# Two of the first loads' sources move to ScalarE's queue: block 1's first token half and the second weight granule

## The chip, the cores and the metric

The kernel runs on one core of a Trainium2 chip. Its five engines work side by side, each through its own instructions in a fixed order: TensorE (PE in the profile, with its weight loads as PEld), VectorE (DVE), ScalarE (ACT), GpSimd (POOL) and SyncE (SP), which here only issues DMAs. A DMA that an engine issues is carried out by 16 DMA engines that all queues of the core share. The metric is the device time of one execution in microseconds (us); lower is better.

## The reference

Two layers of a decoder trunk over 256 tokens of width 1024, all in float32. Each layer is a mixer followed by a gated feed-forward part, both between RMS norms with a residual:

```python
def rmsnorm(x, g):
    y = xf * lax.rsqrt(jnp.mean(xf * xf, axis=-1, keepdims=True) + RMS_EPS)
    return (y * g.astype(F32)).astype(x.dtype)

def hybrid_mixer(h, w_in, ...):
    proj = h @ w_in                       # 1024 x 3088
    aq, ak, av, gq, gk, gv, gr, g_low = jnp.split(proj, cuts, axis=-1)
    ...                                   # attention over aq, ak, av; gated linear attention over the rest
    return mixed @ w_out

def swiglu(h, w_gate, w_up, w_down):
    return (jax.nn.silu(h @ w_gate) * (h @ w_up)) @ w_down

def reference(x, ...):
    h = x
    for l in range(DEPTH):                # DEPTH = 2
        m = hybrid_mixer(rmsnorm(h, mix_pre_norm[l]), ...)
        h = h + rmsnorm(m, mix_post_norm[l])
        f = swiglu(rmsnorm(h, ffn_pre_norm[l]), w_gate[l], w_up[l], w_down[l])
        h = h + rmsnorm(f, ffn_post_norm[l])
    return h
```

## The kernel before

The 256 tokens lie in two blocks of 128 rows, `h[0]` and `h[1]` (h0 and h1 in the profile's order rows: h_87 and h_88). A weight matrix comes in granules of two times 128 rows by 512 columns (512 KB): each granule is loaded into one of four buffers `raw`, and then split for a product of float32 accuracy. ScalarE writes the rounded part `wh`, VectorE the remainder `wl` = weight - `wh`; in the first layer both multiply with a column of the norm's gain, `gcol`, on the way, a row half (128 rows) at a time. Tokens are transposed on TensorE (`tp_x`, four transposes for 512 columns), then split in the same way into `xh_x` (ScalarE) and `xl_x` (VectorE). A product is three matmuls: xh times wh, xh times wl, xl times wh. The first product is `aq`, the queries: 4 granules x 2 row halves x 2 token blocks x 3 = 48 matmuls of 512 columns; granules 0 and 1 need the first 512 columns of the tokens, granules 2 and 3 the last. `gqk`, `ak`, `gr`, `gv`, `av` and `wo` follow, then the feed-forward part.

Before the first product the gain has to be there: `grow`, a 16 x 128 table (8 KB), is loaded, transposed on TensorE (`tp_gain`) and copied by ScalarE into `gcol`. Every `wh` and `wl` of the first granules reads `gcol`. TensorE also runs two bursts of matmuls on zeros, `warm` (`NWARM`, 6 and 3 calls), one before `tp_gain` and one between the first and the second `tp_x`.

The order on each engine is not written by hand. A class `Clock` keeps a modelled time for each engine; generators for the tasks (`first_x`, `highs`, `lows_`, `project`, ...) are woken at modelled times and emit their instructions then. So a change of the first loads also changes what the planner emits next, on all engines, until its modelled times agree again. `Engine.__getattr__` charges every call to the engine's name; all objects named "DMA" share one modelled queue. `load_x(j, i)` (line 1412) loads half i of token block j, `load_plain(i)` (line 338) granule i, and `grow_of` (line 1408) the gain table. The first three granules are loaded as two DMAs of 256 KB each (`NSTEP` = 3). A granule from the fifth on waits for its buffer, that is for the `wl` of the granule four before it. The first loads are issued by lines 1416 to 1424, all on SP's queue.

Of the kernel before, what the change touches and what calls it, by code (L numbers as in the profile page):

```python
# [21 lines left out]
P = 128  # L22
# [34 lines left out]
class Engine:  # L57


    def __init__(self, clock, name, eng):  # L60
        self.clock, self.name, self.eng = clock, name, eng
# [46 lines left out]
class Clock:  # L108
# [5 lines left out]
    def __init__(self, nc):  # L114
        self.at = dict.fromkeys(("PE", "Act", "DVE", "Pool", "DMA"), 0.0)
        self.idle = 0.0
        self.queue = 0.5
        self.free = {}
        self.port = {}
        self.writes = {}  # L120
        self.last = {}
        self.slots = {}
        self.open = set()
        self.tasks = []
        self.pumps = []
        self.count = 0
        self.pe = Engine(self, "PE", nc.tensor)
        self.act = Engine(self, "Act", nc.scalar)
        self.dve = Engine(self, "DVE", nc.vector)
        self.pool = Engine(self, "Pool", nc.gpsimd)  # L130
        self.dma = Engine(self, "DMA", nc.sync)

    @staticmethod
    def span(ap):
# [103 lines left out]
def trunk(ctx: ExitStack, tc: tile.TileContext, io: dict):  # L238
    nc = tc.nc
# [6 lines left out]
    ck = Clock(nc)  # L246
    pe, act, dve, pool, dma, close = ck.pe, ck.act, ck.dve, ck.pool, ck.dma, ck.close
# [54 lines left out]
    for l in range(L):  # L302
        w_in, w_out = io["w_in"][l], io["w_out"][l]
        for name in ("gqk", "aq", "ak", "gr", "gv", "av") if l else ("aq", "gqk", "ak", "gr", "gv", "av"):
            if name == "gqk":
                add((l, name), [w_in[:, 1536:2048], w_in[:, 3072:3088]], 8, 528, None if l else 0)
            else:
                c0 = {"aq": 0, "ak": 512, "gr": 2560, "gv": 2048, "av": 1024}[name]
# [26 lines left out]
    lows = [0]  # L335
    plain_lows = [0]

    def load_plain(i):
        key, k0, kk, n, srcs = queue[i]
        raw = wpool.tile([P, kk, n], F32, tag="raw", bufs=NRAW, name="raw")  # L340
        if len(raws) >= NRAW:
            ck.after(raw, raws[-NRAW])
        step = 1 if len(raws) < NSTEP else kk
        for k in range(0, kk, step):
            c0 = 0
            for src in srcs:
                w = src.shape[1]
                r0 = (k0 + k) * P
                dma.dma_start(raw[:, k:k + step, c0:c0 + w],
                              src[r0:r0 + step * P, :].rearrange("(k p) n -> p k n", p=P))  # L350
                c0 += w
        raws.append(raw)
        raw_of[i] = raw

    def loader(first):
        for what, at_, *src in loads[first:]:
            if what == "plain":
                while len(raws) >= plain_lows[0] + NRAW:
                    yield ck.now() + 0.1
                load_plain(at_)  # L360
                continue
            f = forms[at_]
            while at_[0] not in (mixed_all if what in ("b11", "b21") else sums_of):
                yield ck.now() + 0.1
            t = yield from ck.tile(sb, [P, 4, 512], F32, "big", NBIG, what)
            if src[0] is not None:
                fw = src[0].shape[1]
                for g in range(2):
                    dma.dma_start(t[:, 2 * g:2 * g + 2, 0:fw],
                                  src[0][256 * g:256 * (g + 1), :].rearrange("(k p) n -> p k n", p=P))  # L370
            f["tiles"][what] = t
            if what in ("b11", "b21", "b22"):
                f["ready"][what] = t
# [1009 lines left out]
            then = pre_norm(j, xout, l + 1) if l + 1 < L else None  # L1383
            ck.spawn(post_norm(j, acc[j], gi, then), ck.now())

    act.preload_act_table_set("natural_log_exp_and_others")

    warm = sb.tile([P, P], F32, tag="ra", bufs=1, name="warm")
    dve.memset(warm, 0.0)
# [14 lines left out]
    h = [const.tile([P, D], F32, name=f"h{j}") for j in range(2)]  # L1404
# [3 lines left out]
    def grow_of(name, t):  # L1408
        dma.dma_start(t, io[name].rearrange("l (k p) -> (l k) p", p=P))
        return t  # L1410

    def load_x(j, i):
        c = slice(i * 512, (i + 1) * 512)
        dma.dma_start(h[j][:, c], io["x"][0, j * P:(j + 1) * P, c])

    load_x(0, 0)
    grow = grow_of("mix_pre_norm", sb.tile([16, P], F32, tag="lsig", bufs=1, name="grow"))
    load_plain(0)
    load_x(1, 0)
    load_plain(1)  # L1420
    load_x(0, 1)
    load_x(1, 1)
    for i in range(2, 4):
# [91 lines left out]
```

## Time and profile before

| What | Value |
|---|---|
| Time, three runs | 642.36, 639.14, 641.89 us; median 641.89 us |
| Profiled execution | 639.99 us, its span 638.2 us |
| TensorE busy | 622.1 us, 97% of the span |
| VectorE busy | 504.3 us, 79% |
| ScalarE busy | 412.6 us, 65% |
| GpSimd busy | 23.7 us, 4% |
| Moved by DMA | 109.30 MB, mean 171 GB/s |

All times within the profile count from the start of the span; the execution's own time is 1.8 us longer than its span. Busy is the time in which an engine has an instruction at work; for TensorE the ends of matmuls are modelled, so its 97% says that something was in its pipeline, not that it computed at its peak. A row of a timeline gives start, duration, engine, line, operation, result and sources, and in square brackets how long the engine stood idle before and what released it. Line L77 is the helper through which every operation is recorded, so groups are told apart by their tiles.

### The profile page before, as it was taken

To read this page: it belongs to the slowest core of one execution; us is meant where nothing else is said; L and a number is where in the kernel's file an instruction comes from. 1 tells how busy PE (TensorE), PEld (TensorE's weight loads), DVE (VectorE), ACT (ScalarE), POOL (GpSimd) and SP (SyncE) were. 2 spreads that over 40 slices of the span, in tenths; PEclk is the share of its full clock that TensorE was granted. 3 is DMA by queue.
4 is the path that set the end of the run, shared out by engine and by line. 5 is a ranking of instruction groups with operands and counts; after the bars stand their busy time and mean duration, and the time that the engine had idled before them with its cause. 6 is when DMAs were issued, how large, how long until landed. Compare 5 with 4: busy or idle time off the path is not lost.

```text
span 638.2 us, 10255 instructions
## 1 busy us (share of the span) xinstructions
PE 622.1 (97%) x3896; PEld 510.7 (80%) x3896; DVE 504.3 (79%) x784; ACT 412.6 (65%) x700; POOL 23.7 (4%) x41
## 2 busy tenths in 40 slices
PE   8999999989999999999999999999899999999995
PEld 7987778868888888879788777887788888888894
DVE  4899975579897899987588996557899778989743
ACT  6889855486946385656577797537966555838531
POOL 1000021000000000000010000110000000000000
PEclk9999999979999999999999999999899999999998
DMA  8965455156048946039474714840910895710811
GB/s 281 281 193 156 149 188 191 52 174 255 1 142 294 397 152 201 1 104 289 142 246 149 205 46 126 277 142 17 368 45 3 286 353 216 270 61 1 263 68 66
DMA packets 53108, 109.30 MB, mean 171 GB/s; under 512 B 5890, under 2 KB 10692, under 8 KB 53060
## 3 DMA queue, kind: packets, MB, share of 16 engines
q1 hardware_dynamic: 53060, 108.66, 51.4%
q8 instruction: 30, 0.49, 0.3%
q14 instruction: 18, 0.15, 0.1%
HBM read 107.60 MB, written 1.05 MB: 170 GB/s over the span
## 4 chain that ended last, share of the span: by engine, by line
PE 86%; DVE 5%; DMA 3%; ACT 3%; issue 2%; SPq 1%; POOLq 0%; DVEq 0%; ACTq 0%
PE dn L77 17%; PE seven_a L77 10%; PE gate_ps L77 8%; PE up_ps L77 8%; PE seven_b L77 7%; PE wo L77 4%; PE gr L77 4%; PE gqk L77 4%; PE ak L77 4%; PE gv L77 3%; PE av L77 3%; PE aq L77 3%; DVE wl L77 3%; ACT wh L77 2%; PE att_o L77 2%
## 5 line engine op out<-in xcount | busy, mean ns | idle before, releaser
L77 DVE TENSOR_TENSOR wl<-raw,wh 128x1024 fp32r<-128x1024 f32 (+1 forms) x124 | 150.3, 1221 | 32.4 <-ACT wh L77 31.6
L77 ACT ACTIVATE wh<-raw 128x1024 fp32r<-128x1024 f32 (+1 forms) x124 | 130.0, 1059 | 54.1 <-DMA raw<-w_gate 17.3
L77 ACT ACTIVATE wh<-b 128x1024 fp32r<-128x1024 f32 x72 | 75.0, 1058 | 38.2 <-PE up_ps L77 9.3
L77 DVE TENSOR_TENSOR wl<-b,wh 128x1024 fp32r<-128x1024 f32 x72 | 84.9, 1218 | 2.9 <-ACT wh L77 2.8
L77 PE MATMUL dn<-wh,xh_h 128*128 128x512 f32 x176 | 70.4, 400 | 0.0
L77 PE MATMUL dn<-wl,xh_h 128*128 128x512 f32 x176 | 69.5, 395 | 0.0
L77 PE MATMUL dn<-wh,xl_h 128*128 128x512 f32 x176 | 69.1, 393 | 0.0
L77 DVE TENSOR_TENSOR b<-b,b 128x1024 f32<-128x1024 f32 x36 | 42.7, 1217 | 0.0
L77 POOL TENSOR_TENSOR rstd<-var,nhalf 128x1 f32<-128x1 f32 (+1 forms) x24 | 21.2, 883 | 557.6 <-DVE var L77 557.5
L77 PEld LDWEIGHTS dn<-wl,xh_h 128*128 128x128 f32 x176 | 33.1, 188 | 8.2 <-DVE wl L77 1.4
L77 PEld LDWEIGHTS dn<-wh,xl_h 128*128 128x128 f32 x176 | 33.0, 188 | 7.4
L77 PEld LDWEIGHTS dn<-wh,xh_h 128*128 128x128 f32 x176 | 33.1, 188 | 7.0
L77 DVE SCALAR_TENSOR_TENSOR wl<-raw,gcol,wh 128x512 fp32r<-128x512 f32 (+1 forms) x48 | 34.4, 748 | 1.6 <-ACT wh L77 1.6
L77 ACT ACTIVATE wh<-raw,gcol 128x512 fp32r<-128x512 f32 (+1 forms) x48 | 32.4, 717 | 4.7 <-DMA raw<-w_in 3.3
L77 PE MATMUL gate_ps<-wh,xh_x 128*128 128x512 f32 (+1 forms) x96 | 34.9, 363 | 0.0
L77 PE MATMUL up_ps<-wh,xh_x 128*128 128x512 f32 (+1 forms) x96 | 34.3, 358 | 0.0
L77 PE MATMUL gate_ps<-wh,xl_x 128*128 128x512 f32 (+1 forms) x96 | 34.1, 356 | 0.0
L77 PE MATMUL gate_ps<-wl,xh_x 128*128 128x512 f32 (+1 forms) x96 | 34.1, 355 | 0.0
L77 PE MATMUL up_ps<-wh,xl_x 128*128 128x512 f32 (+1 forms) x96 | 34.1, 355 | 0.0
L77 PE MATMUL up_ps<-wl,xh_x 128*128 128x512 f32 (+1 forms) x96 | 34.1, 355 | 0.0
L77 ACT ACTIVATE xh_h<-tp_h 128x512 fp32r<-128x512 f32 (+1 forms) x24 | 13.3, 554 | 25.1 <-PE tp_h L77 24.9
L77 DVE TENSOR_TENSOR xl_h<-tp_h,xh_h 128x512 fp32r<-128x512 f32 (+1 forms) x24 | 15.5, 645 | 14.9 <-ACT xh_h L77 14.8
(233 smaller groups left out, 1483.9 us busy)
## 6 DMA issues: line engine op xcount, KB each, us to landing
raw<-w_in SPq DMA_DIRECT2D x45, 512.0 KB, 4.6
raw<-w_down SPq DMA_DIRECT2D x44, 512.0 KB, 4.9
b<-w_gate SPq DMA_DIRECT2D x24, 512.0 KB, 8.2
b<-w_up SPq DMA_DIRECT2D x24, 512.0 KB, 7.5
raw<-w_gate SPq DMA_DIRECT2D x20, 512.0 KB, 4.4
raw<-w_up SPq DMA_DIRECT2D x20, 512.0 KB, 4.8
raw<-w_out SPq DMA_DIRECT2D x16, 512.0 KB, 3.7
raw<-w_in SPq DMA_DIRECT2D x6, 256.0 KB, 5.1
```

The lines of the kernel that those rows point to most:

```text
L77: return f(*args, **kw)
```

## The change

A second object named "DMA" is made whose instructions go to ScalarE's queue (`ck.dma2`), and `load_x` and `load_plain` take the queue as an argument. Block 1's first token half and granule 1 (its two row halves) are issued by ScalarE, ahead of its activation-table load, which moves behind them. On SP's queue granule 0 moves ahead of the gain table, and the other loads follow.

```diff
@@ -129,6 +129,7 @@
         self.dma = Engine(self, "DMA", nc.sync)
+        self.dma2 = Engine(self, "DMA", nc.scalar)
@@ -335,7 +336,7 @@
-    def load_plain(i):
+    def load_plain(i, q=dma):
@@ -346,7 +347,7 @@
-                dma.dma_start(raw[:, k:k + step, c0:c0 + w],
+                q.dma_start(raw[:, k:k + step, c0:c0 + w],
                               src[r0:r0 + step * P, :].rearrange("(k p) n -> p k n", p=P))
@@ -1383,7 +1384,6 @@
-    act.preload_act_table_set("natural_log_exp_and_others")
@@ -1409,15 +1409,16 @@
-    def load_x(j, i):
+    def load_x(j, i, q=dma):
         c = slice(i * 512, (i + 1) * 512)
-        dma.dma_start(h[j][:, c], io["x"][0, j * P:(j + 1) * P, c])
+        q.dma_start(h[j][:, c], io["x"][0, j * P:(j + 1) * P, c])
 
     load_x(0, 0)
+    load_x(1, 0, ck.dma2)
+    load_plain(0)
+    load_plain(1, ck.dma2)
+    act.preload_act_table_set("natural_log_exp_and_others")
     grow = grow_of("mix_pre_norm", sb.tile([16, P], F32, tag="lsig", bufs=1, name="grow"))
-    load_plain(0)
-    load_x(1, 0)
-    load_plain(1)
     load_x(0, 1)
     load_x(1, 1)
     for i in range(2, 4):
```

**SP's and ScalarE's first rows.** SP before, from its first DMA on; h_87 is token block 0, h_88 token block 1, and each of these DMAs but `grow` carries 256 KB (the last row 512 KB each):

```order
L77 DMA h_87<-x 128x512
L77 DMA grow<-mix_pre_norm 16x128
L77 DMA raw<-w_in 128x512 x2
L77 DMA h_88<-x 128x512
L77 DMA raw<-w_in 128x512 x2
L77 DMA h_87<-x 128x512
L77 DMA h_88<-x 128x512
L77 DMA raw<-w_in 128x512 x2
L77 DMA raw<-w_in 128x2x512 x2
```

SP with the change, from its first DMA on; the names have moved by one, so h_86 is block 0 and h_87 block 1:

```order
L77 DMA h_86<-x 128x512
L77 DMA raw<-w_in 128x512 x2
L77 DMA grow<-mix_pre_norm 16x128
L77 DMA h_86<-x 128x512
L77 DMA h_87<-x 128x512
L77 DMA raw<-w_in 128x512 x2
L77 DMA raw<-w_in 128x2x512
L77 DMA rope<-rope 128x64
```

The gain table stands fourth instead of second on SP, behind three DMAs of 256 KB, and three DMAs are gone from SP. ScalarE before, from its first instruction on:

```order
L77 ACT_TABLE_LOAD
L77 ACTIVATE gcol<-tp_gain 128x16
L77 ACTIVATE xh_x<-tp_x 128x512
L77 ACTIVATE wh<-raw,gcol 128x512 x3
L77 ACTIVATE xh_x<-tp_x 128x512
L77 ACTIVATE wh<-raw,gcol 128x512
L77 ACTIVATE xh_x<-tp_x 128x512
L77 ACTIVATE wh<-raw,gcol 128x512
L77 ACTIVATE xh_x<-tp_x 128x512
```

ScalarE with the change, from its first instruction on:

```order
L77 DMA h_87<-x 128x512
L77 DMA raw<-w_in 128x512 x2
L77 ACT_TABLE_LOAD
L77 ACTIVATE gcol<-tp_gain 128x16
L77 ACTIVATE wh<-raw,gcol 128x512
L77 ACTIVATE xh_x<-tp_x 128x512
L77 ACTIVATE wh<-raw,gcol 128x512
L77 ACTIVATE xh_x<-tp_x 128x512 x2
L77 ACTIVATE wh<-raw,gcol 128x512 x2
L77 ACTIVATE sq,ms<-h_87 128x1024
L77 ACTIVATE xh_x<-tp_x 128x512
L77 ACTIVATE sq,ms<-h_86 128x1024
```

Three DMA issues stand ahead of the table load, two splits of block 1's tokens run together, and one of the two sums of squares (`sq`) has moved ahead of the last split of block 0's tokens.

**TensorE's and VectorE's first rows.** TensorE before, from its first matmul on:

```order
L77 MATMUL warm<-warm 128x128 x6
L77 MATMUL tp_gain<-ident,grow 128x16
L77 MATMUL tp_x<-ident,h_87 128x128 x4
L77 MATMUL warm<-warm 128x128 x3
L77 MATMUL tp_x<-ident,h_88 128x128 x4
L77 MATMUL aq<-wh,xh_x 128x512
L77 MATMUL aq<-wl,xh_x 128x512
L77 MATMUL aq<-wh,xl_x 128x512
L77 MATMUL aq<-wh,xh_x 128x512
L77 MATMUL aq<-wl,xh_x 128x512
L77 MATMUL aq<-wh,xl_x 128x512
L77 MATMUL tp_x<-ident,h_87 128x128 x4
```

TensorE with the change, from its first matmul on:

```order
L77 MATMUL warm<-warm 128x128 x6
L77 MATMUL tp_gain<-ident,grow 128x16
L77 MATMUL tp_x<-ident,h_86 128x128 x4
L77 MATMUL warm<-warm 128x128 x3
L77 MATMUL tp_x<-ident,h_87 128x128 x8
L77 MATMUL tp_x<-ident,h_86 128x128 x4
L77 MATMUL aq<-wh,xh_x 128x512
L77 MATMUL aq<-wl,xh_x 128x512
```

All four groups of token transposes, the second halves of both blocks too, stand ahead of the first matmul of `aq`; before, two of the four stood behind it. VectorE before, from its second instruction on:

```order
L77 TENSOR_TENSOR xl_x<-tp_x,xh_x 128x512
L77 SCALAR_TENSOR_TENSOR wl<-raw,gcol,wh 128x512 x2
L77 TENSOR_TENSOR xl_x<-tp_x,xh_x 128x512
L77 SCALAR_TENSOR_TENSOR wl<-raw,gcol,wh 128x512 x2
L77 TENSOR_TENSOR xl_x<-tp_x,xh_x 128x512 x2
```

VectorE with the change, from its second instruction on:

```order
L77 TENSOR_TENSOR xl_x<-tp_x,xh_x 128x512 x3
L77 SCALAR_TENSOR_TENSOR wl<-raw,gcol,wh 128x512 x2
L77 TENSOR_TENSOR xl_x<-tp_x,xh_x 128x512
L77 TENSOR_SCALAR var<-ms 128x1
L77 SCALAR_TENSOR_TENSOR wl<-raw,gcol,wh 128x512 x2
```

The `wl` of granule 0 stands behind three token splits instead of one. Further on TensorE's order differs in the first mixer alone, where shorter pieces change places (among them `av`, the gated attention of block 1 and its transposes `tp_g`); from the middle of `wo` of the first layer to the end the order of both programs is the same.

## Rows read from the trace of the kernel before

**Rows 1.** The page, parts 1 and 4: busy time, and the chain that ended last

```profile
PE 622.1 (97%) x3896; PEld 510.7 (80%) x3896; DVE 504.3 (79%) x784; ACT 412.6 (65%) x700; POOL 23.7 (4%) x41
PE 86%; DVE 5%; DMA 3%; ACT 3%; issue 2%; SPq 1%; POOLq 0%; DVEq 0%; ACTq 0%
```

**Rows 2.** Windows: stretch, length, busy us (instructions) by engine, PEclk, DMA share, GB/s

```profile
2.00:5.00 3.00, 3.00 (x15) 2.74 (x14) 0.00 (x0) 0.20 (x2) 0.27 (x1) 1.00 0.92 222
7.50:10.00 2.50, 2.10 (x13) 1.51 (x12) 0.97 (x2) 1.78 (x3) 0.00 (x0) 1.00 1.04 385
20.00:100.00 80.00, 80.00 (x848) 65.04 (x847) 67.87 (x186) 64.56 (x149) 3.64 (x4) 1.00 0.62 199
```

**Rows 3.** The chain that ended last, in order of time: start us, us, what

```profile
4.00 5.52 DMA h<-x
...
11.43 9.03 PE aq L77 x39
20.46 3.30 PE gqk L77 x27
```

**Rows 4.** Timeline of SP's queue from 0 us

```profile
0.74 0.39 SPq L77 DMA_DIRECT2D h<-x  x1
1.18 0.41 SPq L77 DMA_DIRECT2D grow<-mix_pre_norm  x1
1.65 0.88 SPq L77 DMA_DIRECT2D raw<-w_in  x2
```

**Rows 5.** The tile grow, its DMA alone

```profile
DMA to landing us min/median/max: 2.4/2.4/2.4
```

**Rows 6.** Timeline of TensorE, 1 to 21 us

```profile
1.05 2.93 PE L77 MATMUL warm<-warm 128*128 128x128 f32 x12 [1.05 <-DVE warm L77]
3.91 0.28 PE L77 MATMUL tp_gain<-ident,grow 16*128 16x16 f32 x1
4.12 1.11 PE L77 MATMUL tp_x<-ident,h 128*128 128x128 f32 x4
5.03 1.49 PE L77 MATMUL warm<-warm 128*128 128x128 f32 x6
7.61 0.49 PE L77 MATMUL aq<-wh,xh_x 128*128 128x512 f32 x1
9.66 0.63 PE L77 MATMUL tp_x<-ident,h 128*128 128x128 f32 x4 [0.40 <-DMA h<-x]
20.07 0.39 PE L77 MATMUL aq<-wh,xl_x 128*128 128x512 f32 x1
```

**Rows 7.** Timeline of ScalarE, 0 to 21 us

```profile
0.73 1.28 ACT L77 ACT_TABLE_LOAD   x1 [0.73 <-PEq L1503]
4.23 0.18 ACT L77 ACTIVATE gcol<-tp_gain 128x16 f32<-128x16 f32 x1 [2.22 <-PE tp_gain L77]
8.22 0.73 ACT L77 ACTIVATE wh<-raw,gcol 128x512 fp32r<-128x512 f32 x1 [1.13 <-DMA raw<-w_in]
10.32 0.60 ACT L77 ACTIVATE xh_x<-tp_x 128x512 fp32r<-128x512 f32 x1 [0.29 <-PE tp_x L77]
12.61 1.04 ACT L77 ACTIVATE sq<-h 128x1024 bf16<-128x1024 f32 x1
```

**Rows 8.** Timeline of VectorE, 0 to 21 us

```profile
6.51 1.42 DVE L77 SCALAR_TENSOR_TENSOR wl<-raw,gcol,wh 128x512 fp32r<-128x512 f32 x2
11.39 1.43 DVE L77 TENSOR_TENSOR xl_x<-tp_x,xh_x 128x512 fp32r<-128x512 f32 x2
```

**Rows 9.** Timeline of TensorE, late in the first mixer

```profile
107.71 0.66 PE L77 MATMUL tp_g<-ident,gon 128*128 128x128 f32 x4 [0.77 <-DVE gon L77]
```

**Rows 10.** Windows at the two starts of the feed-forward part, columns as in rows 2

```profile
136.20:143.00 6.80, 6.13 (x15) 4.62 (x15) 5.16 (x7) 4.90 (x13) 0.36 (x1) 0.50 0.89 256
450.20:453.60 3.40, 3.40 (x9) 2.63 (x8) 3.13 (x5) 2.40 (x6) 0.00 (x0) 0.50 0.91 311
```

## The prediction

> **What bounds the kernel now.** I read the page's busy table and chain first: TensorE is at work 97% of the span, and 86% of the chain that ended last runs through it [rows 1]. A chain of this kind says that a delay at the start comes out at the end, if TensorE never waits long enough in between to catch it up. So I looked next at windows: from 20 to 100 us TensorE is busy 80.00 of 80.00 us, with VectorE at 67.87 and ScalarE at 64.56 [rows 2]. Nothing there can swallow a delay. The first place with a real wait is at 107.7 us, 0.77 us long [rows 9]. Then the start itself, by the chain in order of time and the three timelines: the chain begins with a DMA, the second half of a token block that is issued at 4.00 and lands at 9.52, and from 11.43 on it is `aq`, 39 matmuls in 9.03 us, 0.2315 us each, which ends at 20.46 where `gqk` takes over [rows 3]. `aq` began at 7.61 and starts its last matmul at 20.07 [rows 6]; 48 matmuls without a hole would need 11.1 us, so it loses 1.6 us to holes and to the two groups of transposes in it. What counts is therefore one number: when the last `aq` matmul starts.
>
> **How the first data arrive.** The gain table lands 2.4 us after its issue at 1.18 [rows 4, 5], at 3.6; `tp_gain` begins at 3.91 and `gcol` at 4.23 [rows 6, 7]. The 256 KB loads behind it land in the order of issue: the first half of granule 1, which is the fourth 256 KB load after the first, lets `wh` begin at 8.22 [rows 7], and the load two places later lands at 9.52 [rows 3], so one load per 0.65 us. That puts the sixth large load (granule 1's second half) at 8.9 and the eighth (block 1's second half) at 10.2. The DMA engines are the limit by then: 385 GB/s at a share of 1.04 between 7.5 and 10 us. Between 2 and 5 us they carry 222 GB/s at a share of 0.92 [rows 2]: held up, though not for want of issues, since SP issues one load per 0.45 us [rows 4].
>
> **The change part by part.**
>
> *The issues.* SP loses three issues of about 0.44 us, ScalarE gains three. On ScalarE they come before the table load: 0.73 + 1.3 + 1.28 = 3.3 us for its end, against 2.0 now [rows 7]. Nothing needs ScalarE before `gcol`, which needs the gain table, so this costs nothing; even with the gain table at its old 3.6 it would be covered, by 0.9 us.
>
> *The gain table.* It is now SP's fourth DMA, behind block 0's first half and both halves of granule 0, while ScalarE's queue holds three loads of the same size. No row shows two queues loaded at once, so I bound it. At best only SP's own queue counts: the first load lands by 3.6, two more at 0.65 us each, 4.9. At worst all six loads come first at today's pace: 8.9. If the second queue fills the slow stretch, 3 us x (385 - 222) GB/s = 0.49 MB are won, 1.3 us at 385 GB/s: 7.6. Both queues are filled from 0.74 us at one pace, so I take the six, with most of that gain: 7.8. The eighth large load, with the same 1.1 us gained, lands at 9.1 (bounds 8.9 to 10.2): its place in the bytes has not changed.
>
> The Trainium skill (DMA: Bandwidth & Descriptors, "Queues, rings and completion order") says that each DMA engine takes turns between the queues that have work, and under "Issuing engines are not separate DMA queues" that issuing from several engines saves only issue time. By these the gain table stays behind all six loads and nothing of the slow stretch is won: 8.9, and the sum below grows by 1.1 us. No run here has shown it yet.
>
> *From the gain table to the first `aq` product.* Every step has a row. `tp_gain` 0.3 after the landing: 8.1. The second `warm` burst ends 2.6 after that start (3.91 to 6.52 today [rows 6]): 10.7, and only then block 1's first transposes. Their `xh_x` starts 0.66 later (9.66 to 10.32 [rows 6, 7]), 11.36; the second `xh_x` in the pair at 11.96, to 12.56. VectorE now has three `xl_x` ahead of `wl`; the third ends 0.7 after its `xh_x` (two take 1.43 [rows 8]): 13.25. The first `wl` of granule 0 takes 0.71 (two in 1.42 [rows 8]): 13.95. It ends at 7.2 today. The second matmul of `aq` cannot start before 13.95. The first matmul, ahead of it, waits for nothing later than that.
>
> *One more hole.* ScalarE goes on after 12.56 with two `wh` (1.4, to 14.0), then `sq` of block 1 (1.04 [rows 7], to 15.0), then the last `xh_x` (to 15.6); VectorE's `xl_x` of it (16.3) and the first `wl` of granule 1 (17.0) follow. TensorE reaches that granule's second matmul, the 14th, at 13.95 + 12 x 0.2315 = 16.7 and gets it at 17.05. From there 34 starts more: 17.05 + 34 x 0.2315 = 24.9 for the last `aq` start, against 20.07: **4.9 us later**. With 4.9 for the gain table the eighth load decides: landed at 8.9, `xh_x` at 9.9, `wl` ends 11.85, 2.1 us earlier, so 2.8 us later than today in all. With 8.9 it is 6.0.
>
> *The next granules.* The fifth load now stands behind three smaller ones on SP and waits for the `wl` of granule 0, ended at 14.7. With a landing some 5.5 us later (4.00 to 9.52 [rows 3]) it is there at 20.2 and split by 23, ahead of 25. No second wait. The later granules follow at the pace of `wl`, as now.
>
> *Rest of the first mixer.* The pieces that change places are the same work; TensorE is full there, so they cost nothing unless one comes before its data. At 107.7 us the wait of 0.77 us may go, because block 1's gated attention now stands earlier against `av`. I take half: -0.4, between -0.8 and, if such a wait appears elsewhere, +0.8.
>
> *TensorE's clock.* The first four `tp_x` take 1.11 us, later ones 0.63 [rows 6]: the array runs at its lower level (1.2 GHz) at first, though the column of the windows has 1.00 there [rows 2]. Today `warm`, `tp_gain` and `tp_x` keep it at work from 1.05 to 6.5. With the change it stands idle from 4.0 (end of the first `warm` burst) to 8.1, then works to 10.7 and again has holes up to 13.95. So `aq` may begin at 1.2 GHz. The rows show low stretches of 6.8 and 3.4 us at a granted 0.50 [rows 10]. From nothing (high before 13.95) to 6.8 us low from there, half of it lost: 0 to +3.4; I take +0.6, nearer to none, since the second burst and 12 transposes run before.
>
> **The sum.** +4.9 - 0.4 + 0.6 = +5.1 us on the profiled execution's 639.99 us (span 638.2): 645.1. That execution lies 1.9 below the median of the three timed ones, 641.89; the four average 640.9. I add to the average: **646.0 us**.
>
> **Rivals.**
>
> *The gain table slips through.* If SP's queue is served before ScalarE's, it lands near 4.9 and the eighth load decides: +2.8 - 0.4 + 0.6, 643.9. For it: a table of 8 KB needs no bandwidth. Against: three large loads stand ahead in the same queue, and today's loads land in order of issue.
>
> *The clock stays low into `aq`.* +4.9 - 0.4 + 3.4: 648.8. For it: 4.1 us of idleness where none was. Against: `warm` runs again right before.
>
> *Nothing is lost.* The delay is caught up before the end: some wait that the windows do not show gives it back, about 641. Against it stands the full TensorE from 20 to 100 us.
>
> *Faster.* The start costs 2.8, and the two low stretches at 136 and 450 us are missed, because the feed-forward parts begin at another moment: they cost 6.8 / 2 = 3.4 and 3.4 / 2 = 1.7 us [rows 10], and 0.8 us comes from 107.7: 640.9 + 2.8 - 5.1 - 0.8 = 637.8. For it: two starts of the same kind have low stretches of different length, so their length is not fixed. Against: the order of work ahead of them is as before, and both stretches have to go. To come out faster (below 638.7, see below) more than 640.9 + 2.8 - 0.8 - 638.7 = 4.2 of these 5.1 us must be won; less only softens the loss.
>
> **How the numbers follow.** My forecast has 0.50 (643.5 to 648.5 by itself), the gain table that slips through 0.20, the low clock 0.17, nothing lost 0.07, faster 0.06. A measurement of this kernel can tell about 0.5%, 3.2 us, from no change: faster is below 638.7, slower above 645.1. Slower: three quarters of the forecast, all of the low clock, a fifth of the first rival, 0.58. Faster 0.07, with a little for the timed runs' own scatter of 3.2 us; no change 0.35. The range runs from 641 to 650, from nothing lost to the low clock with the table at 8.9.
>
> **What would show it.** Right: `gcol` starts near 8.4 instead of 4.23; TensorE idle from 4.0 to 8; the first `wl` of granule 0 ends near 14; the last `aq` start near 25; from there TensorE's rows of the first mixer follow in the same distance, and `wo` ends some 4 to 5 us later. Wrong: `gcol` at 5 to 6 (the queues are not shared evenly), a first `aq` before 11, or `aq` late but the start of the feed-forward part not later.

## The result, and the profile after

The changed kernel takes 644.63 us (median of 18 runs, 641.24 to 647.62); the kernel before, on the same chip, 640.66 us (18 runs, 638.42 to 644.39). The ratio is 1.0064 with a 95% interval of 1.0049 to 1.0080: slower by 4.1 us, between 3.1 and 5.1. The forecast was 646.0.

The profiled execution took 643.37 us (span 641.6), 3.4 more than the one of before. Its busy times are those of before [rows 1], to within 1 us per engine:

```profile
PE 621.5 (97%) x3896; PEld 510.8 (80%) x3896; DVE 503.6 (79%) x784; ACT 412.0 (64%) x700; POOL 22.7 (4%) x41
```

So nothing became dearer; TensorE did the same work later. The beginning, first by the queues. SP's queue, timeline of the changed kernel (start us, us, what):

```profile
0.74 0.38 SPq L77 DMA_DIRECT2D h<-x  x1
1.18 0.89 SPq L77 DMA_DIRECT2D raw<-w_in  x2
2.11 0.43 SPq L77 DMA_DIRECT2D grow<-mix_pre_norm  x1
```

ScalarE, the same stretch and on to its first activation:

```profile
0.73 0.41 ACTq L77 DMA_DIRECT2D h<-x  x1
1.17 0.93 ACTq L77 DMA_DIRECT2D raw<-w_in  x2
2.14 1.28 ACT L77 ACT_TABLE_LOAD   x1 [2.14 <-issue]
8.52 0.18 ACT L77 ACTIVATE gcol<-tp_gain 128x16 f32<-128x16 f32 x1 [5.10 <-PE tp_gain L77]
```

The two queues do issue side by side, and the table load ends at 3.42, long before anything needs ScalarE. The chain in order of time says what the start now hangs on:

```profile
2.11 5.99 DMA grow<-mix_pre_norm
8.10 0.14 issue
8.23 0.25 PE tp_gain L77
8.48 1.04 PE tp_x L77 x4
9.53 1.28 PE warm L77 x6
10.81 1.72 PE tp_x L77 x8
12.55 0.60 ACT xh_x L77
```

Before, the chain began with a 256 KB token load [rows 3]. Now it is the gain table, 8 KB, 5.99 us from issue to landing (2.4 before [rows 5]). TensorE's timeline shows what follows from it:

```profile
8.23 0.25 PE L77 MATMUL tp_gain<-ident,grow 16*128 16x16 f32 x1 [4.25 <-DMA grow<-mix_pre_norm]
...
13.49 0.48 PE L77 MATMUL aq<-wh,xh_x 128*128 128x512 f32 x1
14.59 0.50 PE L77 MATMUL aq<-wl,xh_x 128*128 128x512 f32 x1 [0.62 <-DVE wl L77]
...
25.37 0.39 PE L77 MATMUL aq<-wh,xl_x 128*128 128x512 f32 x1
```

The last `aq` matmul starts at 25.37 against 20.07 [rows 6], 5.3 us later. From the second `aq` matmul on they follow at about 0.23 us without a hole: (25.37 - 14.59) / 46 starts = 0.234. VectorE shows why the second matmul waits until 14.59: three `xl_x` stand ahead of the first `wl`, which ends at about 14.5.

```profile
10.20 0.69 DVE L77 TENSOR_TENSOR xl_x<-tp_x,xh_x 128x512 fp32r<-128x512 f32 x1 [9.20 <-ACT xh_x L77]
12.33 0.69 DVE L77 TENSOR_TENSOR xl_x<-tp_x,xh_x 128x512 fp32r<-128x512 f32 x1 [1.44 <-ACT xh_x L77]
13.18 0.69 DVE L77 TENSOR_TENSOR xl_x<-tp_x,xh_x 128x512 fp32r<-128x512 f32 x1 [0.16 <-ACT xh_x L77]
13.79 1.41 DVE L77 SCALAR_TENSOR_TENSOR wl<-raw,gcol,wh 128x512 fp32r<-128x512 f32 x2
```

How the delay goes on is read from one tile. The products `seven_a` stand in both feed-forward parts; the two numbers behind the durations are the starts of the first and of the last of these 48 instructions. Changed kernel:

```profile
L77 PE MATMUL seven_a<-wh,xh_x x48: 387/395/628, 141.5 to 593.4; 128*128 128x512 f32 x48
```

Before:

```profile
L77 PE MATMUL seven_a<-wh,xh_x x48: 389/395/628, 135.7 to 589.9; 128*128 128x512 f32 x48
```

So the delay is 5.3 us at the end of `aq`, 5.8 at the start of the first feed-forward part and 3.5 near the end of the second. Four things lie between. TensorE, full from 20 to 100 us before [rows 2], now has three waits there:

```profile
28.29 0.63 PE L77 MATMUL tp_heads<-ident,qk_sb 128*128 128x128 f32 x4 [0.35 <-DVE qk_sb L77]
...
35.97 0.27 PE L77 MATMUL ltp<-ident,qks 128*17 128x128 f32 x1 [0.77 <-ACT qks L77]
...
65.27 0.97 PE L77 MATMUL score<-khl,q 64*128 64x256 f32 x6 [0.37 <-DVE nmax L77]
```

Together they are 1.5 us. The wait of 0.77 us at 107.7 [rows 9] is gone: `tp_g` follows `av` at once (108.62 + 0.23 = 108.85).

```profile
108.62 0.39 PE L77 MATMUL av<-wh,xl_x 128*128 128x512 f32 x1
108.85 0.60 PE L77 MATMUL tp_g<-ident,gon 128*128 128x128 f32 x4
```

The low stretch (a stretch at a granted clock of about 0.5) at the first feed-forward part is 3.4 us instead of 6.8 [rows 10]; the one at the second part is 3.4 us long, as it was. What the first is worth can be read from two starts, the first `seven_a` on `xh_x` and the first on `sums_h`: they lie 32.85 us apart before (135.66 to 168.51) and 31.53 with the change (141.53 to 173.06), 1.3 us less. The second of these rows, before and then with the change:

```profile
168.51 0.40 PE L77 MATMUL seven_a<-wh,sums_h 128*128 128x512 f32 x1
```

```profile
173.06 0.40 PE L77 MATMUL seven_a<-wh,sums_h 128*128 128x512 f32 x1
```

Windows of the changed kernel (columns as in rows 2):

```profile
2.00:5.00 3.00, 1.98 (x10) 1.69 (x8) 0.00 (x0) 1.28 (x1) 0.28 (x1) 1.00 0.87 267
...
14.00:16.00 2.00, 1.41 (x6) 1.14 (x7) 1.27 (x3) 2.00 (x5) 0.00 (x0) 1.00 0.00 0
20.00:100.00 80.00, 78.51 (x830) 63.42 (x830) 68.06 (x189) 64.00 (x147) 1.84 (x4) 1.00 0.57 175
...
142.60:146.00 3.40, 3.02 (x7) 2.44 (x8) 3.39 (x5) 2.39 (x6) 0.00 (x0) 0.51 0.94 330
```

And the profile of before has a wait on TensorE that the changed one has not:

```profile
306.79 0.44 PE L77 MATMUL tp_h<-ident,sg 128*128 128x128 f32 x2 [1.00 <-DVE sg L77]
```

5.3 + 1.5 - 0.8 - 1.3 - 1.0 = 3.7, against 3.4 by the two spans; the rest lies in smaller differences. Which of these belong to the change, and which to the single execution, the experiments have to say.

### The profile page after: what moved, and what is told of

Same layout as the page of the kernel before. It is cut to its first block, busy times and chain, and to the rows that moved or that the text cites. A ratio compares the mean times of both kernels' runs of the same rounds, so it can differ in the third digit from the quotient of the medians.

```text
span 641.6 us, 10253 instructions
## 1 busy us (share of the span) xinstructions
PE 621.5 (97%) x3896; PEld 510.8 (80%) x3896; DVE 503.6 (79%) x784; ACT 412.0 (64%) x700; POOL 22.7 (4%) x41
## 4 chain that ended last, share of the span: by engine, by line
PE 87%; DVE 4%; ACT 4%; DMA 2%; issue 2%; SPq 0%; POOLq 0%; DVEq 0%; ACTq 0%
PE dn L77 19%; PE seven_a L77 11%; PE gate_ps L77 9%; PE up_ps L77 9%; PE seven_b L77 8%; PE wo L77 4%; PE gv L77 4%; PE av L77 3%; PE gr L77 3%; PE gqk L77 2%; PE ak L77 2%; PE aq L77 2%; DVE wl L77 2%; PE att_o L77 2%; ACT wh L77 2%
```

## Experiments

Each ratio is against runs of the kernel before on the same chip. The change does three things at once: two loads go through another queue, the gain table moves from second to fourth place on SP's, and the order in which the engines split tokens and weights changes with the planner's due times. The diffs leave out what they share with the change (`ck.dma2` and the queue argument). My theory was that the late gain table makes the loss and the queues as such nothing; the rival was that the second queue itself costs.

**The queues alone.** The kernel before, with the gain table still second on SP, and the two loads on ScalarE's queue, ahead of its table load. The engines' order is that of before.

```diff
-    load_x(1, 0)
-    load_plain(1)
+    load_x(1, 0, ck.dma2)
+    load_plain(1, ck.dma2)
+    act.preload_act_table_set("natural_log_exp_and_others")
```

> Order of every compute engine as before the change; only block 1's first half and granule 1 are issued by ScalarE, and the gain table stays SP's second DMA. Theory (the loss is the gain table's late landing and the engines' order that follows from it): the gain table lands near 4, the last aq start lies between 19 and 20.5 us, the time is that of the kernel before, -1 to +0.5 us. Rival (a second queue itself slows the first loads, by sharing the DMA engines): the loads on SP land later, the time is 2 to 4 us above before.

Measured: 640.26 us (12 runs) against 640.51 (23), ratio 1.0000 (0.9977 to 1.0022). The rival falls. TensorE's timeline:

```profile
5.46 0.26 PE L77 MATMUL tp_gain<-ident,grow 16*128 16x16 f32 x1 [1.49 <-DMA grow<-mix_pre_norm]
...
20.84 0.39 PE L77 MATMUL aq<-wh,xl_x 128*128 128x512 f32 x1
```

The gain table is second on SP in both kernels and lands at 5.33 here, at 3.6 before, where I had expected it near 4: the other queue's loads take their part of the same DMA engines. The Trainium skill (DMA: Bandwidth & Descriptors, "Queues, rings and completion order") says that the engines take turns between queues that have work, and the trace agrees by these 1.7 us: with SP's queue served first the table would have landed as before. Under "Issuing engines are not separate DMA queues" it says that issuing from several engines saves only issue time; that too agrees, by the ratio of 1.0000. The last `aq` starts at 20.84, 0.77 later than before and above the 19 to 20.5 that I had expected; the time does not show it within its interval.

**The order alone.** The changed kernel, all loads on SP's queue.

```diff
-    load_x(1, 0, ck.dma2)
+    load_x(1, 0)
     load_plain(0)
-    load_plain(1, ck.dma2)
+    load_plain(1)
```

> Order of every compute engine as with the change, but all loads on SP's queue, in the order of the changed code: the gain table is the seventh DMA there. Theory: the gain table lands at 8.9 (six large loads at the pace of the kernel before), the first wl of granule 0 ends near 15.3, the time is 4.5 to 6 us above before, about 1 us above the change. Rival (the second queue makes the loss): the time is that of before, within 1 us.

Measured: 647.91 us (6 runs), ratio 1.0094 (1.0061 to 1.0126). The gain table is now seventh in one queue, issued at 3.53, and its product starts at 8.93:

```profile
8.93 0.25 PE L77 MATMUL tp_gain<-ident,grow 16*128 16x16 f32 x1 [4.95 <-DMA grow<-mix_pre_norm]
...
25.59 0.39 PE L77 MATMUL aq<-wh,xl_x 128*128 128x512 f32 x1
```

The last `aq` starts at 25.59, 0.22 later than with two queues. The whole loss is there without the second queue. Whether that queue wins back anything in time is not settled: the two intervals overlap, and the traces speak for 0.2 us. The profiled execution is the shortest of the six, 642.55 us; only its start is read here.

**The gain table late, the order of before.** One queue, the table's DMA issued behind both granules; the planner books it where it was, so that the engines' order stays.

```diff
-    grow = grow_of("mix_pre_norm", ...)
+    grow = sb.tile(...)
+    gsrc = io["mix_pre_norm"].rearrange(...)
+    ck.note("DMA", dma.cost("dma_start", [grow], {}), [gsrc], [grow])
     load_plain(0)
     load_x(1, 0)
     load_plain(1)
+    nc.sync.dma_start(grow, gsrc)
```

> Order of every compute engine as before the change, one queue; the gain table is issued behind granule 1, as SP's seventh DMA. Theory: it lands near 8.9, the first wl of granule 0 ends near 12, and as all tokens and granules 0 to 2 have landed by then aq runs without a hole: last start near 23.7, 3 to 5 us above before. Rival (the engines' order alone makes the loss): within 1 us of before.

Measured: 645.72 us (6 runs), ratio 1.0077 (1.0055 to 1.0099), 4.9 us (3.5 to 6.3).

```profile
8.55 0.25 PE L77 MATMUL tp_gain<-ident,grow 16*128 16x16 f32 x1 [4.58 <-DMA grow<-mix_pre_norm]
...
24.25 0.39 PE L77 MATMUL aq<-wh,xl_x 128*128 128x512 f32 x1
```

The late table alone costs 4.2 us at the last `aq`, and the time follows.

**The gain table early, the order of the change.** The changed kernel, with the table's DMA issued second on SP and booked at its late place.

```diff
     load_x(0, 0)
+    grow = sb.tile(...)
+    gsrc = io["mix_pre_norm"].rearrange(...)
+    nc.sync.dma_start(grow, gsrc)
     load_x(1, 0, ck.dma2)
     load_plain(0)
     load_plain(1, ck.dma2)
-    grow = grow_of("mix_pre_norm", ...)
+    ck.note("DMA", dma.cost("dma_start", [grow], {}), [gsrc], [grow])
```

> Order of every compute engine and both queues as with the change, but the gain table is issued as SP's second DMA, as before the change. Theory: the table lands near 4.5 and no longer decides; block 1's second half (the eighth large load) does: it lands near 8.9 to 9.3, the first wl of granule 0 ends near 12, the last aq start near 23, the time is 1.5 to 3 us above before. Rival 1 (the gain table alone makes the loss): within 0.7 us of before. Rival 2 (the engines' order alone makes it): as the change, 4 us above.

Measured: 644.58 us (12 runs), ratio 1.0051 (1.0031 to 1.0070), 3.3 us (2.0 to 4.5), a little above what I had expected. Here the table is early, as in the prediction's rival of the table that slips through. As that rival said, the eighth load then decides:

```profile
5.41 0.26 PE L77 MATMUL tp_gain<-ident,grow 16*128 16x16 f32 x1 [1.43 <-DMA grow<-mix_pre_norm]
...
9.51 0.63 PE L77 MATMUL tp_x<-ident,h 128*128 128x128 f32 x4 [0.66 <-DMA h<-x]
...
12.21 0.54 PE L77 MATMUL aq<-wl,xh_x 128*128 128x512 f32 x1 [0.89 <-DVE wl L77]
...
24.51 0.39 PE L77 MATMUL aq<-wh,xl_x 128*128 128x512 f32 x1
```

The last `aq` is 4.4 us late, of which some 1.6 come from a low stretch that this execution has in `aq`: between 12.55 and 15.96 eight starts take 3.41 us, 0.43 apart instead of 0.23. Without it 2.8, as in the prediction.

```profile
12.50:15.90 3.40, 3.40 (x9) 2.64 (x9) 2.67 (x7) 3.40 (x8) 1.05 (x2) 0.51 0.55 155
```

So the late table and the order each hold back the same `aq` matmuls. By the last start they cost 4.2 and 2.8 us by themselves and 5.3 together: they do not add, since one delay hides most of the other. The times (4.9, 3.3 and 4.1 us) have intervals too wide to rank them. Part of the 3.3 is the clock: an estimate like the one at the end of this section leaves 2.6.

**The table load first.** The queues alone, with ScalarE's table load ahead of its DMAs.

```diff
-    load_x(1, 0)
-    load_plain(1)
+    load_x(1, 0, ck.dma2)
+    load_plain(1, ck.dma2)
```

The table load stays where the kernel before has it, ahead of all loads.

> Order of every compute engine as before the change; ScalarE issues block 1's first half and granule 1, but behind its table load, so from about 2.0 us on; the gain table is SP's second DMA. Theory (two queues fill the slow stretch of the DMA engines between 3 and 5 us, but delay the gain table when both start together): the gain table lands at 3.6 as before, the eighth large load near 9 instead of 10.2, the last aq start between 19.0 and 19.8 us, the time 0.2 to 1 us below before, too little to tell. Rival (the slow stretch is not filled by a second queue): last aq start at 20.1, the same time.

Measured: 640.75 us (12 runs) against 641.53 (23), ratio 0.9994 (0.9975 to 1.0014). The last `aq` starts at 20.67, where I had expected 19.0 to 19.8. The experiment did not do what I had meant. The DMAs did not wait for the table load:

```profile
0.73 1.28 ACT L77 ACT_TABLE_LOAD   x1 [0.73 <-PEq L1504]
0.76 0.39 ACTq L77 DMA_DIRECT2D h<-x  x1
```

So there was no delay to measure, and it is a second run of the queues alone, with the same answer.

**The gain table planned early.** The changed kernel, with the one line that loads the table moved to its old place, so that the planner sees it early too.

```diff
     load_x(0, 0)
+    grow = grow_of("mix_pre_norm", ...)
     load_x(1, 0, ck.dma2)
     load_plain(0)
     load_plain(1, ck.dma2)
     act.preload_act_table_set("natural_log_exp_and_others")
-    grow = grow_of("mix_pre_norm", ...)
```

> The change with one line moved: the gain table is issued and planned as SP's second DMA, both queues stay. The planner then puts aq ahead of the second halves' transposes again. Theory: the loss of the change goes; the gain table lands near 5.2, the last aq start is near 20.8 as with the queues alone, the time within 1 us of before. The shorter pieces late in the first mixer keep the order of the change, so this also tells what that order is worth: theory nothing beyond 1 us. Rival (the order late in the first mixer carries a part of the loss): 1.5 us or more above before.

Measured: 642.75 us (12 runs) against 641.53 (23), ratio 1.0017 (0.9998 to 1.0035), 1.1 us, where the change costs 4.1.

```profile
8.48 0.78 PE L77 MATMUL aq<-wh,xh_x 128*128 128x512 f32 x1
10.90 0.50 PE L77 MATMUL aq<-wl,xh_x 128*128 128x512 f32 x1 [1.64 <-DVE wl L77]
...
22.53 0.39 PE L77 MATMUL aq<-wh,xl_x 128*128 128x512 f32 x1
```

Most of the loss goes with this one line. I had expected the last `aq` at 20.8; it starts at 22.53, since two `xl_x` still stand ahead of the first `wl` on VectorE and TensorE waits 1.64 us for it. Late in the mixer the pieces stand as in the changed kernel, so that part of the new order carries no loss that this can see. It carries a gain, less 0.2 us at `score`: the wait of 0.77 us at 107.7 is gone here too, as in all profiled kernels with the changed order late in the mixer, and the queues alone, the late table and the table load first, which have the old order, still show 0.76 or 0.77.

**Both kernels profiled a second time**, to tell the change from the single execution.

> The changed kernel once more, for a second profile. Theory: gain table at about 8.1 us again; the wait of TensorE for gqk's weights between 27 and 36 us (1.4 us in the first profile) hangs on a late DMA and may be shorter or missing; the wait of 1.2 us that the kernel before has at 305 us and the first profile of the change has not is chance and may be there. Rival: both belong to the change and stay.

> The kernel before once more, for a second profile. Theory: the start as in the first profile within 0.1 us up to 40 us; the low clock at the start of the first feed-forward part (6.8 us in the first profile) is 3.4 us as in the other kernels, and the wait at 305 us may be missing. Rival: both are there again, so that they belong to the kernel before and the change wins them back.

The changed kernel took 646.19 us, the one before 640.6. The start repeats in the changed one to 0.03 us:

```profile
8.20 0.26 PE L77 MATMUL tp_gain<-ident,grow 16*128 16x16 f32 x1 [4.22 <-DMA grow<-mix_pre_norm]
...
25.34 0.39 PE L77 MATMUL aq<-wh,xl_x 128*128 128x512 f32 x1
```

In the kernel before `tp_gain` is again at 3.91, but the last `aq` starts 0.37 us earlier than in the first profile, against my expectation of 0.1:

```profile
19.70 0.39 PE L77 MATMUL aq<-wh,xl_x 128*128 128x512 f32 x1
```

So the delay at the last `aq` is 5.3 us in the first pair of profiles and 5.6 in the second. The wait at 107.7 is in both executions of before (0.77, 0.76 us) and in neither of the changed kernel: that gain belongs to the change. So does the wait of 0.37 us for `score`, which the second profile of the changed kernel has again and neither of before. The rest differs between executions of one kernel. The two waits around `gqk` are absent from the second profile of the changed kernel, although the DMA engines stand still there too from 14 to 16 us. The wait of 1.00 us at 306.79 is absent from the second profile of before, and the second of the changed kernel has one of 1.01 us, at 313.05. And a long low stretch, which the first profile of the changed kernel lacks, is in its second, but at 94 us; the kernel before has its own at 136 again, where I had expected 3.4 us:

```profile
94.30:101.10 6.80, 6.80 (x24) 5.32 (x24) 5.13 (x9) 5.36 (x15) 0.00 (x0) 0.50 0.53 187
```

```profile
136.50:143.30 6.80, 6.08 (x15) 4.79 (x15) 5.12 (x8) 4.90 (x13) 0.17 (x1) 0.50 0.92 280
```

Over all timed runs the mean granted clock is 0.988 for both kernels (18 runs of the changed one, and the 23 of the one before beside the first four experiments). This gives an estimate of what the clock is worth: the time at the lower level is 2 x (1 - clock) x span, and taking half of it from each span leaves 635.3 us for the changed kernel and 631.0 for the one before: 4.4 us apart, against 3.9 between the spans' means. By this estimate the clock carries none of the loss.

## Why the prediction was right

**The gain table** was the step on which the sum stood. I took a landing at 7.8, between 4.9 and 8.9; it landed at 8.10. That ScalarE's loads take their share ahead of it is shown by the queues alone, where the table's place on SP is that of before and it lands 1.7 us later. That the six loads set it is shown by the two runs with the table behind all six in one queue: 3.53 + 4.89 = 8.42 (the late table) and 3.53 + 5.26 = 8.79 (the order alone). So the second queue won 0.3 to 0.7 us at this landing, not the 1.1 that I took.

**From the table to `aq`**: `gcol` was forecast at 8.4 and started at 8.52; the third `xl_x` ended at 13.87 (13.25), the last `aq` started at 25.37 (24.9). Of the 0.6 us missing at the `xl_x`, 0.1 is the landing and 0.5 lies in block 1's transposes: the first `xh_x` behind them started at 11.70 instead of 11.36, and I spaced the two 0.6 us apart, where they came 0.85 apart (11.70, 12.55). The hole at the 14th matmul, which I put at 17.05, closed by itself: with the second matmul at 14.59 the 14th came at 17.45, and the weights were there. Term: +4.9 forecast, +5.3 and +5.6 measured in the two pairs of profiles.

**The wait at 107.7** went altogether, where I took half: -0.4 forecast, -0.8 measured.

**The clock**: +0.6 forecast, 0 measured. Neither profile of the changed kernel has a low stretch in `aq`, nor has the order alone; the run with the early table, which has the same order, shows that it can happen, at some 1.6 us for 3.4. Of the forecast's rivals this one keeps some truth. How often it happens, profiles of single executions do not tell.

**"No second wait"** failed as a step. The fifth load itself held: its second `wl` ends at 22.07, ahead of `gqk` at 25.60. What failed is that the later granules would follow as they did before. The first profile has 1.1 us of waits around `gqk`: the next loads are issued only at 15.28, when the first two `wl` are done (13.79 + 1.41 = 15.2), the DMA engines move nothing between 14 and 16 us, and ScalarE then waits for the next three granules, 1.38 us at 22.26, 1.50 at 25.13 and 1.12 at 28.77, where its waits for the weights of `gqk` were 0.90 at most before:

```profile
28.77 1.37 ACT L77 ACTIVATE wh<-raw,gcol 128x528 fp32r<-128x528 f32 x2 [1.12 <-DMA raw<-w_in]
```

The second profile of the same kernel has that idle stretch but no wait of TensorE there. The cover exists but is thin. The 0.37 us for `score`, in both, I had not seen at all. With these waits the last `wo` matmul of the first layer starts 5.9 us later (132.98 to 138.84), where I had 4 to 5.

**The sum** of what belongs to the change: 5.3 + 0.4 - 0.8 + 0 = 4.9 us (5.2 with the second pair's 5.6), at the upper end of the measured 3.1 to 5.1; I had 5.1. That the two sums agree so well is partly luck: the clock's share and the half wait were too high, the start and the waits behind it too low, and they cancel. The path was right: the table, then `aq`, then a TensorE that stays nearly full.

**One reading rested on a single profile.** I took the 222 GB/s between 2 and 5 us [rows 2] as room that a second queue might fill. The second profile of the kernel before carries 247 there. The changed kernel has 267; with one queue, the order alone has 269 and the late table 293:

```profile
2.00:5.00 3.00, 1.98 (x10) 1.68 (x8) 0.00 (x0) 0.01 (x1) 0.28 (x1) 1.00 0.98 293
```

So a second queue is not what this stretch needed, and of the 45 GB/s between 222 and 267, 25 are the scatter of the kernel before. Whether the small table in second place holds the stream up, no run here tells from that scatter.

## What to carry to other kernels

Before a load is moved between queues, look for the smallest transfer that the first dependent instruction needs and count the bytes ahead of it in all queues, not in its own: here 8 KB that land 4.8 us late are enough, by themselves, for a loss as large as the change's (the late table: 4.2 us at the last `aq`, 4.9 in time). A load that moves also moves the planner's view of when its users are due, and that order alone cost 3.3 us with the table early, so test the transfer and the order apart. And where TensorE has no idle time for 80 us behind the start, a delay of 4 or 5 us there comes out at the end; the 0.77 us of the queues alone was too little for the runs to tell.

## What was not expected of the hardware

- A DMA on ScalarE's queue behind a table load in program order was issued while that load ran: table load from 0.73 to 2.01, issue at 0.76.
- An 8 KB load takes 2.4 us from issue to landing as second on SP alone, 3.9 to 4.1 with a loaded second queue (queues alone, table load first, table early), and 5.99 and 5.95 as fourth with both loaded (the two profiles of the changed kernel).
- With both queues loaded SP needs 2.72 us to issue the two token loads behind the gain table (2.58 to 5.30); with all loads on SP's own queue the same two take 0.90 (4.00 to 4.90, the order alone).
- Low stretches of TensorE's clock (granted 0.50 or 0.51) come in lengths of 3.4 and 6.8 us at other places in two executions of one program: 142.6 and 453.2 in the first profile of the changed kernel, 94.3, 145.5 and 456.1 in the second. 3.4 us of it cost some 1.6 us within `aq` (the early table) and 1.3 at the start of the first feed-forward part, and the timed runs of one kernel scatter by about 6 us in 640. Why the long one stood at 136 us in both profiles of the kernel before, but not when only its queues were changed, stays open.
